# Two transformer blocks on one core: set-up and modulation sums moved into the second FFN, the last gates ahead of their gelu branch, weight splits at a raised priority

## The chip, the cores and the metric

The program runs on one core of a Trainium2 chip. The time is that of one execution on the device, in microseconds (us); lower is better. TensorE (PE) does matrix products, VectorE (DVE) and ScalarE (ACT) the elementwise work, GpSimd (POOL) set-up work, and SyncE (SP) issues most of the transfers from the chip's memory (DMA).

## The reference

A sequence of 256 positions with 1024 features, in float32, goes through a first block of two layers and then through a second block:

```python
for i in range(DEPTH):                       # first_block, DEPTH = 2
    h = rms_norm(x, norm_mix[i])
    x = x + (mixer_a(...) if i == 0 else mixer_b(...))
    h = rms_norm(x, norm_ffn[i])
    x = x + conv_ffn(h, f_w_up[i], f_conv_w[i], f_conv_b[i], f_w_down[i])
return rms_norm(x, norm_final)

mod = jax.nn.silu(c) @ ada_w[l] + ada_b[l]   # second_block
sh1, sc1, gt1, sh2, sc2, gt2 = jnp.split(mod[:, None, :], 6, axis=-1)
xn = _rmsnorm(h, mix_norm_g[l]) * (1.0 + sc1) + sh1
...                                          # sparse attention, a recurrence, gates
h = h + gt1 * (merged @ w_out[l])
xn2 = _rmsnorm(h, moe_norm_g[l]) * (1.0 + sc2) + sh2
h = h + gt2 * moe(xn2)                       # 32 experts
```

mixer_b is a gated linear recurrence: a gelu branch, a short convolution, two sigmoid gates per head, a scan, a projection out. conv_ffn projects 1024 features to 2 times 3072 (gate and value), runs a 3-tap convolution, multiplies gelu(gate) by value and projects back. The modulation `mod` has six vectors of 1024 (v = 0 to 5), which depend on the small input `c` alone and not on the sequence; v = 0 and 1 are wanted at the second mixer's start, v = 2 behind it, and v = 3, 4 and 5 at the experts.

## The kernel before

**Products.** Every weight is split into two parts of reduced precision, and one product becomes three matmuls (`mm3`, L272, L273, L274). A piece of weights is loaded into a ring of raw places (10 from the first FFN on), ACT copies its high part (L305), DVE subtracts to get the low part (L306), both into a ring of four split places (`arena_r_78` to `arena_r_81`; half-size pieces take `arena_r_82` and `arena_r_83` too). `wload` does this for each piece.

**Order.** The code is written once through; a tile scheduler gives each engine one fixed list of instructions, ranked by a priority that follows the order in which the code emits them. Each engine runs its list strictly in order. `tc.high_priority(n)` ranks what stands inside it as if it had been emitted n instructions earlier.

**Stages.** mixer_a, the first FFN, mixer_b, the second FFN, the final norm, the second mixer, the experts. An FFN has 13 steps: step s computes 256 gate and 256 value columns into the pool "ps" of PSUM (L272 and on), the convolution runs on DVE (L521), and gelu, product (L551) and split follow; from step 1 the projection back accumulates into the four banks of the pool "pc", which are all held until the FFN's ending. There the residuals (L420, four tiles) are added, the next norm's gain is multiplied (L1382 behind the second FFN), PE turns the tiles over (L377), and ACT sums squares (L334).

mixer_b runs four rounds P: `conv_in` (projection, convolution), `gelu_in` (the gelu branch), `recur` of the round before (L633 to L643: exp, tanh, sqrt and scans), `gates` (two gates per head, Tanh L621), then the projection out.

**Modulation.** `mod_load` loads a half vector of ada_w (4 loads of 0.5 MB on SP's queue). With `summed` DVE makes a weighted sum of eight rows (one L795, seven L797) into a buffer "msum", of which there are four; otherwise PE does that in `mod_steps` (L810, eight instructions per half). `mod_steps` then sums over the partitions on PE (L828 for v below 2 and v = 3 and 4, L817 for v = 2 and 5) into a bank of the pool "pc", which DVE adds to the bias (L830, L818):

```python
part = self.mod_scope.tile([128, 512], name="msum", bufs=4)
...
ps, by = psum(), self.sel4
...
ps, c0 = psum(), v * D + 512 * h
```

It handles whatever has been loaded since its last call: the FFNs call it at step 0, mixer_b at P = 0, and `final_norms` behind the second FFN. Before, v = 4 is loaded in mixer_b without `summed`, v = 3 and 5 in the second FFN with it.

**Set-up of block 2.** `setup2` stands between mixer_b and the second FFN: masks and tables (DVE L184, L888 to L905), a write of an image `x_img` and four small transposes on PE (L195, L909).

## Time and profile before

| | |
|---|---|
| time, median of 3 runs | 1501.51 us (1500.48 to 1504.97) |
| profiled execution: own time, span | 1502.12 us, 1500.4 us |
| granted TensorE clock, mean | 0.950 of 2.4 GHz |
| PE busy, share | 1371.2 us, 91% |
| DVE busy, share | 852.7 us, 57% |
| ACT busy, share | 615.2 us, 41% |
| POOL busy, share | 32.2 us, 2% |

The profiled execution is one run of the same program with the hardware profiler on; the span is the time from its first to its last instruction. A busy share is an average over all stages. In the profiled execution mixer_b runs from about 366 to 500 us, the second FFN from 508 to 727 us, the second mixer from 741 us and the experts from about 1040 us to the end.

### The profile page before, as it was taken

The numbers are of one execution on the slowest core, as the hardware profiler recorded it, in microseconds if no ns is written. First come the engines' busy times: TensorE is split into PE (matmuls) and PEld (weight loads), VectorE is DVE, ScalarE is ACT, GpSimd is POOL, SyncE is SP. The second block draws the span as 40 slices with busy tenths as digits, with TensorE's granted clock in tenths as the row PEclk, the third lists the DMA queues.
The fourth block names the chain that finished last, engine by engine and source line by source line (L and its number), as shares of the span: only waits on it lengthen the run. The fifth ranks groups of instructions, "written<-read, shape, count | busy, mean of one in ns | idle before, by whom it ended". The sixth has DMA issues, their size and how long they took to land.

```text
span 1500.4 us, 22885 instructions
## 1 busy us (share of the span) xinstructions
PE 1371.2 (91%) x9085; PEld 1042.1 (69%) x9085; DVE 852.7 (57%) x1628; ACT 615.2 (41%) x955; POOL 32.2 (2%) x63
## 2 busy tenths in 40 slices
PE   7999999999999899999999899998978878879785
PEld 6778999999998689999798688887413313234131
DVE  5796798778788789878859742775201101101011
ACT  6644555556688555555575544552100000000000
POOL 3000000000001000000000100001000000000000
PEclk9999999999999999999899795999999989999998
DMA  9898586555555578563243352487999999999997
GB/s 318 282 327 277 158 274 215 187 187 160 170 182 184 172 272 275 187 191 109 72 153 113 99 121 86 170 336 308 390 421 420 420 420 421 421 421 419 421 419 253
DMA packets 165573, 391.18 MB, mean 261 GB/s; under 512 B 19440, under 2 KB 101100, under 8 KB 141780
## 3 DMA queue, kind: packets, MB, share of 16 engines
q1 hardware_dynamic: 153124, 383.64, 70.2%
q10 hardware_dynamic: 11136, 4.53, 1.3%
q0 software_dynamic: 1200, 1.49, 0.4%
q8 instruction: 73, 1.20, 0.3%
q14 instruction: 40, 0.33, 0.1%
HBM read 386.19 MB, written 3.43 MB: 260 GB/s over the span
## 4 chain that ended last, share of the span: by engine, by line
PE 58%; DMA 29%; DVE 7%; ACT 4%; issue 2%; SPq 0%; POOL 0%; DVEq 0%; ACTq 0%
DMA arena<-expert_w_gate 12%; PE ps L272 9%; PE ps L273 9%; PE ps L274 9%; DMA arena_w<-expert_w_gate 7%; DMA arena_w<-expert_w_down 6%; PE pc L273 5%; PE pc L272 5%; PE pc L274 5%; DMA arena<-expert_w_down 3%; PE pg L272 2%; PE pg L274 2%; PE pg L273 2%; DVE arena_r L306 2%; ACT arena_r L305 1%
## 5 line engine op out<-in xcount | busy, mean ns | idle before, releaser
L305 ACT ACTIVATE arena_r<-arena 128x1024 fp32r<-128x1024 f32 (+2 forms) x330 | 328.9, 1008 | 287.1 <-PE ps L273 73.1
L306 DVE TENSOR_TENSOR arena_r<-arena,arena_r 128x1024 fp32r<-128x1024 f32 (+2 forms) x330 | 376.9, 1154 | 119.2 <-ACT arena_r L305 115.8
L272 PE MATMUL ps<-arena_r,arena_r 128*128 128x256 f32 (+2 forms) x1192 | 353.7, 297 | 1.0 <-DVE arena L818 1.0
L273 PE MATMUL ps<-arena_r,arena_r 128*128 128x256 f32 (+2 forms) x1192 | 352.9, 296 | 1.1 <-DVE arena_r L306 1.1
L274 PE MATMUL ps<-arena_r,arena_r 128*128 128x256 f32 (+2 forms) x1192 | 352.4, 296 | 0.6 <-DVE arena_r L306 0.6
L272 PEld LDWEIGHTS ps<-arena_r,arena_r 128*128 128x128 f32 (+1 forms) x1192 | 229.3, 192 | 10.4 <-issue 3.5
L273 PEld LDWEIGHTS ps<-arena_r,arena_r 128*128 128x128 f32 (+1 forms) x1192 | 229.2, 192 | 7.2 <-DVE arena_r L306 1.5
L274 PEld LDWEIGHTS ps<-arena_r,arena_r 128*128 128x128 f32 (+1 forms) x1192 | 229.2, 192 | 5.6 <-DVE arena_r L306 0.8
L1709 PE MATMUL pc<-arena 128*32 128x512 f32 x576 | 144.4, 672 | 34.1 <-DMA arena<-expert_w_up 18.9
L272 PE MATMUL pc<-arena_r,arena_r 128*128 128x512 f32 x344 | 136.0, 399 | 5.3 <-ACT arena_r L305 3.4
L273 PE MATMUL pc<-arena_r,arena_r 128*128 128x512 f32 x344 | 135.9, 395 | 0.4 <-DVE arena_r L306 0.4
L274 PE MATMUL pc<-arena_r,arena_r 128*128 128x512 f32 x344 | 134.2, 393 | 0.0
L1709 PE MATMUL pc<-arena_w,arena 128*32 128x512 f32 x448 | 117.4, 663 | 15.8 <-DMA arena_w<-expert_w_gate 9.8
L1716 DVE TENSOR_TENSOR arena<-arena,pc 128x512 f32<-128x512 f32 x8 | 5.5, 688 | 204.6 <-PE pc L1709 204.6
L1692 ACT ACTIVATE arena<-ps,mod_col,moe_g 128x128 f32<-128x128 f32 x32 | 14.7, 458 | 246.1 <-DVE arena L1694 246.1
L1709 PEld LDWEIGHTS pc<-arena 128*32 128x32 f32 x576 | 31.4, 120 | 99.1 <-issue 37.1
L272 PE MATMUL pg<-arena_r,arena_r 128*128 128x256 f32 (+1 forms) x312 | 95.0, 306 | 2.0 <-DVE arena L916 1.8
L273 PE MATMUL pg<-arena_r,arena_r 128*128 128x256 f32 (+1 forms) x312 | 94.7, 305 | 1.1 <-DVE arena_r L306 1.1
L274 PE MATMUL pg<-arena_r,arena_r 128*128 128x256 f32 (+1 forms) x312 | 95.1, 306 | 0.2 <-DVE arena_r L306 0.2
L521 DVE SCALAR_TENSOR_TENSOR arena<-arena 128x255 f32<-128x255 f32 (+2 forms) x228 | 94.4, 477 | 0.2
L1735 PE MATMUL pc<-arena 128*32 128x512 f32 (+2 forms) x320 | 74.7, 584 | 11.5 <-DMA arena<-expert_w_down 7.6
L272 PEld LDWEIGHTS pc<-arena_r,arena_r 128*128 128x128 f32 x344 | 65.2, 190 | 19.8 <-ACT arena_r L305 5.1
(451 smaller groups left out, 1688.2 us busy)
## 6 DMA issues: line engine op xcount, KB each, us to landing
arena<-f_w_up SPq DMA_DIRECT2D x96, 512.0 KB, 3.9
arena<-expert_w_gate SPq DMA_DIRECT2D x41, 1024.0 KB, 19.9
arena<-expert_w_down SPq DMA_DIRECT2D x34, 1024.0 KB, 19.9
arena_w<-expert_w_up SPq DMA_DIRECT2D x33, 1024.0 KB, 19.9
arena<-expert_w_up SPq DMA_DIRECT2D x31, 1024.0 KB, 19.9
arena_w<-expert_w_down SPq DMA_DIRECT2D x26, 1024.0 KB, 19.9
arena<-ada_w SPq DMA_DIRECT2D x48, 512.0 KB, 5.6
arena<-f_w_down SPq DMA_DIRECT2D x48, 512.0 KB, 4.2
```

What stands on the lines that cost most here:

```text
L272: nc.tensor.matmul(acc, ah, bh, start=first, stop=False, **kw)
L273: nc.tensor.matmul(acc, ah, bl, start=False, stop=False, **kw)
L274: nc.tensor.matmul(acc, al, bh, start=False, stop=last, **kw)
L305: self.nc.scalar.activation(hi, src, AF.Copy)
L306: self.nc.vector.tensor_tensor(lo, src, hi.bitcast(F32), ALU.subtract)
L521: nc.vector.scalar_tensor_tensor(o[:, i:], src[:, :S - i], w[k - 1 - i], o[:, i:], op0=ALU.mult, op1=ALU.add)
L1692: nc.scalar.activation(xg[:, k], ps[:, j], AF.Identity, scale=g, bias=sh)
L1709: nc.tensor.matmul(gu[i][es], xg[:, kk, es], ws[e][:, k], start=kk == 0, stop=kk == 7, skip_group_check=True)
L1716: tt(hd, hd, gu[1], ALU.mult)
L1735: nc.tensor.matmul(o[es], hT[:, k0 + k, es], ws[e][:, k, f0 - c0:f0 - c0 + n], start=k0 + k == 0, stop=k0 + k == 3, skip_group_check=True)
```

## The change

It does five things. (1) The two split instructions of `wload` are ranked 3000 places ahead. (2) In mixer_b's round P = 2 the gates are emitted ahead of the gelu branch. (3) mixer_b loads no modulation; v = 3, 4 and 5 are all loaded in the second FFN, all with DVE sums (v = 4 was summed on PE). (4) The second FFN calls `mod_steps` at steps 0, 6 and 12 instead of at 0 alone. (5) `setup2` is called at step 8 of the second FFN instead of ahead of it.

```diff
--- before.py
+++ after.py
@@ -216,7 +216,7 @@
         return t
 
 
-    PIECE, WPIECE = 1024, 2048
+    PIECE, WPIECE, URGENT = 1024, 2048, 3000
 
     def ring(self, raw, split):
 
@@ -252,7 +252,8 @@
             raw = self.load_raw(src[:, a0:a0 + m])
             o = self.place("split")
             parts = [view(self.ar.cols(o + i * self.PIECE, m * b), (m, b), F32R) for i in range(2)]
-            self.split_act(parts[0], parts[1], raw)
+            with self.tc.high_priority(self.URGENT):
+                self.split_act(parts[0], parts[1], raw)
             out += [(parts[0][:, i], parts[1][:, i]) for i in range(m)]
         return out
 
@@ -550,7 +551,7 @@
                     nc.scalar.activation(gf, gf, AF.Gelu_apprx_tanh)
                     nc.vector.tensor_tensor(gf, gf, vf, ALU.mult)
                     self.split_act(flat(hd[s][0]), flat(hd[s][1]), gf)
-                if s == 0:
+                if s in ((0,) if layer == 0 else (0, 6, 12)):
                     self.mod_steps()
                 if 1 <= s <= 10:
                     acc = acc or self.banks()
@@ -650,11 +651,14 @@
                     xb, xs = conv_in(P)
                 if P == 0:
                     self.mod_steps()
-                if P < 3:
+                if P < 2:
                     gg = gelu_in(P)
                 y = recur(P - 1, *todo, 4 if P < 3 else 2) if P > 0 else None
                 if P < 3:
-                    todo = (xb, gg, *gates(P, xs))
+                    rg = gates(P, xs)
+                    if P == 2:
+                        gg = gelu_in(P)
+                    todo = (xb, gg, *rg)
                 side(P)
                 if P > 0:
                     acc = acc or self.banks()
@@ -744,11 +748,16 @@
             ss = self.mixer_a(hT, ahead, factors, before, loads({2: (1, 0, 1), 3: (1, 1, 1)}), then(0))
             self.ring(10, 4)
             ss = self.ffn(hT, ss, 0, loads({1: (0, 0, 1), 3: (0, 1, 1), 6: (2, 0, 1), 9: (2, 1, 1)}), then(1))
-            ss = self.mixer_b(hT, ss, loads({0: (4, 0), 1: (4, 1)}), then(2))
-            self.setup2()
+            ss = self.mixer_b(hT, ss, lambda step: None, then(2))
             final, banks = Scope(self), []
-            ss = self.ffn(hT, ss, 1, loads({1: (3, 0, 1), 3: (3, 1, 1), 5: (5, 0, 1), 8: (5, 1, 1)}),
-                          lambda half: self.final_half(final, half, banks))
+            late = loads({1: (3, 0, 1), 2: (3, 1, 1), 3: (4, 0, 1), 4: (4, 1, 1), 6: (5, 0, 1), 7: (5, 1, 1)})
+
+            def beside(s):
+                late(s)
+                if s == 8:
+                    self.setup2()
+
+            ss = self.ffn(hT, ss, 1, beside, lambda half: self.final_half(final, half, banks))
             self.final_norms(final, ss, banks)
```

Lines of the changed kernel stand one further down from L256 on and nine further from L765 on: its L306 and L307 are L305 and L306 of before, L421 is L420, L635 to L644 stand for L634 to L643, L804 and L806 are L795 and L797, L837 and L839 are L828 and L830, L826 and L827 are L817 and L818, L1391 is L1382.

**DVE near the end of mixer_b.** The place is the last round's recurrence (L635), with the set-up of block 2 behind it; `arena` and `arena_r` are working storage and the split ring. Before:

```order
L184 MEMSET arena 128x128
L635 SCALAR_TENSOR_TENSOR arena<-arena 128x512
L306 TENSOR_TENSOR arena_r_79<-arena,arena_r_79 128x1024
L635 SCALAR_TENSOR_TENSOR arena<-arena 128x512
L306 TENSOR_TENSOR arena_r_80<-arena,arena_r_80 128x1024
L888 TENSOR_SCALAR arena<-m_d_4600,m_fr_4601 128x64
L889 TENSOR_SCALAR arena<-m_d_4600,m_fr_4601 128x64
L897 MEMSET arena 128x256
L893 CAST m_fr_4601<-m_ir_4599 128x1
L901 TENSOR_SCALAR arena<-m_d_4600,m_hi_4603 128x64
L894 TENSOR_SCALAR arena<-m_fr_4601 128x1
```

After, at the same recurrence (L636 there):

```order
L636 SCALAR_TENSOR_TENSOR arena<-arena 128x512
L806 SCALAR_TENSOR_TENSOR arena<-arena 128x512 x2
L307 TENSOR_TENSOR arena_r_79<-arena,arena_r_79 128x1024
L307 TENSOR_TENSOR arena_r_80<-arena,arena_r_80 128x1024
L307 TENSOR_TENSOR arena_r_83<-arena,arena_r_83 128x512
L806 SCALAR_TENSOR_TENSOR arena<-arena 128x512
L307 TENSOR_TENSOR arena_r_81<-arena,arena_r_81 128x1024
L636 SCALAR_TENSOR_TENSOR arena<-arena 128x512
L604 TENSOR_TENSOR arena<-ps_4261,arena 128x512
L806 SCALAR_TENSOR_TENSOR arena<-arena 128x512
L638 SCALAR_TENSOR_TENSOR arena<-arena 128x512
L806 SCALAR_TENSOR_TENSOR arena<-arena 128x512
```

The set-up's instructions (L888 and on) are gone from here, and modulation sums (L806) stand between the splits (L307) and the recurrence. In all, 28 such sums and the 4 that begin them (L804) stand between the first FFN's and mixer_b's residuals, where none stood; 19 and 2 of them come behind the first operation (L636) of round 1's recurrence. In the second FFN, which had 28 and 4, there remain 14 and 2.

**PE in step 0 of the second FFN.** `ps` is the FFN's product, `pc_4779` the norm factors spread over the partitions (L354), `pc_4803` the modulation v = 4 (L810, then L828). Before:

```order
L274 MATMUL ps_4644<-arena_r_76,arena_r_80 128x256
L354 MATMUL pc_4779<-arena,ones 128x128
L810 MATMUL pc_4803<-arena 32x512
L354 MATMUL pc_4779<-arena,ones 128x128
L810 MATMUL pc_4803<-arena 32x512 x7
L272 MATMUL ps_4843<-arena_r_76,arena_r_81 128x256
L273 MATMUL ps_4843<-arena_r_77,arena_r_81 128x256
L274 MATMUL ps_4843<-arena_r_76,arena_r_81 128x256
L272 MATMUL ps_4843<-arena_r_76,arena_r_81 128x256
L273 MATMUL ps_4843<-arena_r_77,arena_r_81 128x256
L274 MATMUL ps_4843<-arena_r_76,arena_r_81 128x256
L828 MATMUL pc_4813<-arena 64x1 x8
```

After:

```order
L275 MATMUL ps_4570<-arena_r_76,arena_r_80 128x256
L355 MATMUL pc_4705<-arena,ones 128x128
L273 MATMUL ps_4729<-arena_r_76,arena_r_81 128x256
L274 MATMUL ps_4729<-arena_r_77,arena_r_81 128x256
L275 MATMUL ps_4729<-arena_r_76,arena_r_81 128x256
L273 MATMUL ps_4729<-arena_r_76,arena_r_81 128x256
L355 MATMUL pc_4705<-arena,ones 128x128
L274 MATMUL ps_4729<-arena_r_77,arena_r_81 128x256
```

The 16 instructions of L810 are gone altogether; the 16 of L828 for v = 4 are gone from here and stand at the end of the second FFN, so that 32 of them stand there instead of 16: 16 between its last ten matmuls and 16 behind them. The five transposes of `setup2` (L195, L909), which stood directly ahead of the first matmul of this FFN, now stand some 950 rows further down.

**DVE at the end of the second FFN.** `pc_4972` and `pc_4974` of before and `pc_4860` of after are the FFN's last accumulators. Before:

```order
L420 TENSOR_TENSOR arena<-arena,pc_4973 128x512
L1382 TENSOR_TENSOR arena<-arena 128x512
L420 TENSOR_TENSOR arena<-arena,pc_4972 128x512
L1382 TENSOR_TENSOR arena<-arena 128x512
L420 TENSOR_TENSOR arena<-arena,pc_4974 128x512
L830 TENSOR_TENSOR mod_col<-mod_col,pc_6736 64x8
L1382 TENSOR_TENSOR arena<-arena 128x512
L830 TENSOR_TENSOR mod_col<-mod_col,pc_6746 64x8
L306 TENSOR_TENSOR arena_r_78<-arena,arena_r_78 128x864
```

After, from the first addition into `mod_col` but one:

```order
L307 TENSOR_TENSOR arena_r_78<-arena,arena_r_78 128x864
L839 TENSOR_TENSOR mod_col<-mod_col,pc_5709 64x8
L839 TENSOR_TENSOR mod_col<-mod_col,pc_5719 64x8
L806 SCALAR_TENSOR_TENSOR arena<-arena 128x512
L307 TENSOR_TENSOR arena_r_80<-arena,arena_r_80 128x888
L839 TENSOR_TENSOR mod_col<-mod_col,pc_5729 64x8
L806 SCALAR_TENSOR_TENSOR arena<-arena 128x512
L804 TENSOR_SCALAR arena<-arena 128x512
L806 SCALAR_TENSOR_TENSOR arena<-arena 128x512 x10
L421 TENSOR_TENSOR arena<-arena,pc_4860 128x512
L806 SCALAR_TENSOR_TENSOR arena<-arena 128x512
L1391 TENSOR_TENSOR arena<-arena 128x512
```

Ahead of the last residual (L421 with `pc_4860`) there now stand all four additions into `mod_col` (L839) and most of the sums of v = 5 (L804, L806); before, it stood ahead of both additions and had no sums near it.

Beside these: ACT has three more table loads in mixer_b; its third weight split at the kernel's start stands ahead of the first normalised block (L366); and in the second mixer some matmuls change places.

## Rows read from the trace of the kernel before

**Rows 1.** Windows: busy us (instructions) of each engine, clock, DMA share, GB/s.

```profile
366.00:440.00 74.00, 73.42 (x563) 69.44 (x562) 63.33 (x110) 57.11 (x92) 0.00 (x0) 1.00 0.51 158
440.00:500.00 60.00, 56.24 (x359) 49.83 (x358) 51.26 (x81) 46.22 (x65) 5.65 (x11) 1.00 0.62 202
500.00:508.00 8.00, 4.85 (x25) 2.97 (x25) 6.83 (x20) 6.76 (x16) 0.00 (x0) 0.94 0.56 187
508.00:534.00 26.00, 26.00 (x181) 20.58 (x181) 13.68 (x39) 9.67 (x13) 0.00 (x0) 0.89 0.62 206
534.00:728.00 194.00, 193.98 (x1344) 181.43 (x1344) 166.88 (x242) 108.98 (x143) 2.58 (x6) 0.99 0.58 188
741.00:1040.00 299.00, 279.80 (x2493) 249.94 (x2494) 190.33 (x466) 155.59 (x297) 11.88 (x13) 0.89 0.51 169
```

**Rows 2.** Waits of PE in mixer_b, 366 to 500 us: total, times, longest.

```profile
PE pc L272 <- ACT arena_r L305: 3.4, 2, 1.7
...
PE pc L273 <- DVE arena_r L306: 0.4, 1, 0.4
```

**Rows 3.** Timeline of ACT at the start: start us, us, what [idle before <-releaser].

```profile
10.40 1.06 ACT L305 ACTIVATE arena_r<-arena 128x1024 fp32r<-128x1024 f32 x1 [0.66 <-DMA arena<-a_w_in]
```

**Rows 4.** Modulation sums on DVE: one timeline row, two source rows (ns min/median/max).

```profile
570.11 2.07 DVE L797 SCALAR_TENSOR_TENSOR arena<-arena 128x512 f32<-128x512 f32 x3
...
L797 DVE SCALAR_TENSOR_TENSOR arena<-arena x70: 737/746/756, 77.0 to 611.2; 128x512 f32<-128x512 f32 x70
...
L795 DVE TENSOR_SCALAR arena<-arena x10: 478/482/489, 61.9 to 585.4; 128x512 f32<-128x512 f32 x10
```

**Rows 5.** Timeline of DVE at the set-up of block 2 in mixer_b.

```profile
480.92 0.26 DVE L888 TENSOR_SCALAR arena<-m_d,m_fr 128x64 f32<-128x64 f32 x1 [1.97 <-DMA x_img<-arena]
```

**Rows 6.** Timeline of ACT at a table load in mixer_b.

```profile
423.07 1.28 ACT L604 ACT_TABLE_LOAD   x1
424.36 0.63 ACT L604 ACTIVATE arena<-arena 128x512 f32<-128x512 f32 x1
```

**Rows 7.** Timeline of PE at the step into the second FFN.

```profile
503.74 0.25 PE L195 MATMUL ps<-ident,arena 43*128 43x43 f32 x1
504.03 0.53 PE L909 MATMUL ps<-ident,arena 128*8 128x128 f32 x2
507.08 0.76 PE L909 MATMUL ps<-ident,arena 128*8 128x128 f32 x2 [2.52 <-DVE arena_r L367]
```

**Rows 8.** Timeline of PE in step 0 of the second FFN.

```profile
520.15 0.28 PE L272 MATMUL ps<-arena_r,arena_r 128*128 128x256 f32 x1
...
520.82 1.04 PE L810 MATMUL pc<-arena 128*32 128x512 f32 x2
...
522.22 1.92 PE L810 MATMUL pc<-arena 128*32 128x512 f32 x14
...
526.98 3.18 PE L810 MATMUL pc<-arena 128*32 128x512 f32 x16
...
531.37 2.08 PE L828 MATMUL pc<-arena 128*64 128x1 f32 x16
...
535.13 0.41 PE L274 MATMUL ps<-arena_r,arena_r 128*128 128x256 f32 x1
```

**Rows 9.** Timeline of PE at the end of the second FFN.

```profile
726.89 0.40 PE L274 MATMUL pc<-arena_r,arena_r 128*128 128x512 f32 x1
...
727.66 3.55 PE L828 MATMUL pc<-ones,arena 128*64 128x1 f32 x32
...
740.84 0.55 PE L272 MATMUL ps<-arena_r,arena_r 128*128 128x256 f32 x1 [1.01 <-DVE arena L818]
```

**Rows 10.** Timeline of DVE at the end of the second FFN.

```profile
727.33 0.69 DVE L420 TENSOR_TENSOR arena<-arena,pc 128x512 f32<-128x512 f32 x1 [0.74 <-PE pc L274]
...
729.85 0.68 DVE L1382 TENSOR_TENSOR arena<-arena 128x512 f32<-128x512 f32 x1
...
731.44 1.06 DVE L306 TENSOR_TENSOR arena_r<-arena,arena_r 128x864 fp32r<-128x864 f32 x1
```

## The prediction

> **What bounds the kernel now.** I read the page first, then a table of windows by stage, the waits of TensorE (PE), and the timelines at the places that the change touches. The page's shares (PE 91%, the vector engine, DVE, 57%) hide the stages. The table of windows [rows 1] shows PE full in the second FFN (26.00 of 26 us from 508 to 534, 193.98 of 194 us from 534 to 728), nearly full in the first 74 us of mixer_b (73.42), and with holes at the end of mixer_b (56.24 of 60 us) and at the step into the second FFN (4.85 of 8); the step out of it, 14 us without an FFN matmul, is in a timeline [rows 9]. In mixer_b DVE is busy for 63.33 of 74 and then 51.26 of 60 us, so it is close to being a second bound there. In the second FFN it is busy for 166.88 of 194 us and PE does not wait: there work taken off PE is therefore time, and work taken off DVE is not. The expert stage behind is bound by transfers, but its loads are released by PE's work ahead of it, so I count a shift of PE before the experts one to one at the end.
>
> All terms are made against the profiled execution: its own time is 1502.12 us, its span 1500.4 us; the median of the runs shown is 1501.51 us, so 0.6 us comes off at the end. A plus is slower.
>
> **The change, part by part.**
>
> *Weight splits first.* In mixer_b PE waits for the two halves of a split: 3.4 us in two waits for the ACT copy (L305) and 0.4 us for the DVE subtract (L306) [rows 2]. Splits that go ahead of other work can remove these: 3.8 us, less if DVE is late anyway. At the kernel's start the third split now stands ahead of the first normalised block, L366, on ACT. One such copy is 1.06 us and before it ACT waited 0.66 us for its weights [rows 3], so the first matmul comes 0 to 1.7 us later; I take +1.3, nearer to the full price.
>
> *Modulation sums of v=3 and v=4 in mixer_b.* The order of after has 28 of the seven-per-half L797 and 4 of the one-per-half L795 between mixer_b's start and its first residual, where before had none of them: they were summed in the second FFN (v=3) or on PE (v=4). A run of three L797 takes 2.07 us, of which the third needs 0.75, so the pitch is 0.66; an L795 is 0.48 alone, and I take 0.40 by the same overlap [rows 4]. The set-up's DVE work leaves mixer_b: L888 (0.26 us) and ten small ones behind it and a memset, some 2 us (an estimate from the first row, with overlap), and with them a wait of 1.97 us for the write of x_img [rows 5].
> In the last 60 us DVE idles 60 − 51.26 = 8.7 us; 19 of the L797 and 2 of the L795 now stand there, 19 × 0.66 + 2 × 0.40 = 13.3 us. The idle time and the 2 us removed hold 10.7, so DVE is late by 2.6 us even if it never waits. It will wait: it depends on ACT and PE in this stretch. Of the idle time, 1.97 us is the x_img wait that goes; of the remaining 6.8 I keep half, 3.4 us. DVE's end of mixer_b, and with it the residual that PE's next transposes need, is then 2.6 + 3.4 = 6.0 us late. Against this stands the 3.8 us of split waits that no longer hold up PE's chain: +2.2. The bounds are −3.8 (all sums fit) and +13.3 (none does). The other 9 L797 and 2 L795, 6.7 us, meet 74 − 63.33 = 10.7 us of idle DVE and cost nothing. Their loads move too: 8 loads of ada_w, 0.5 MB each, leave the second FFN for mixer_b's part of SP's queue. There 0.62 of the engines' time moves 202 GB/s [rows 1], so full engines would move some 326 (an estimate) and 4 MB need 13 us; 0.38 of 60 us and 0.49 of 74 are free, 59 us, and I cost them at nothing.
>
> *Gates ahead of the last gelu branch.* The same matmuls in another order, and three more activation table loads on ACT, 1.28 us each [rows 6], 3.8 us. ACT is idle for 60 − 46.22 = 13.8 us in the last 60 us, so I cost them at nothing; without that cover they would be 3.8.
> The Trainium skill ("ScalarE: Activation LUTs", section on what a table load costs) puts a switch of tables at about 2.66 us, 1.28 of it the load and the rest a drain, and advises to group by table, which speaks against this edit. The trace agrees with the 1.28 but shows the activation 0.01 us behind the end of the load [rows 6]: no drain there. By the page's figure the three would be an estimated 8.0 us.
>
> *Set-up of block 2 moves behind.* At the step into the second FFN PE waits 2.52 us ahead of the last two of the L909 transposes [rows 7]; the four L909 and the L195 are gone from there. The matmuls then run at the lower clock of 1.2 GHz: 0.41 us instead of 0.28 for each record [rows 8], from 507.73 to about 510.4; PE had been idle for 3.15 of the 8 us around it. At the full rate these 2.7 us would be about half; without the hole I take 1.2 us back: −3.7 together (bounds −1.0 and −5.6). Inside the FFN the same five transposes cost their own 0.25 + 0.53 + 0.76 us: +1.5 (bounds +1.0, and +4.0 if the 2.5 us wait comes with them).
>
> *Modulation v=4 off PE.* In step 0 of the second FFN PE runs 32 records of L810, 1.04 + 1.92 + 3.18 us, and 32 of L828 in two groups of 2.08 us each [rows 8]. Spans overlap by 0.1 or 0.2 us, so L810 is 5.9 us and L828 4.0. PE is full there: −9.9. A second low-clock stretch follows, with matmuls of 0.41 us from 534.5 to 537.7 [rows 8]; with dense matmuls ahead of it in place of thin ones, it goes: −1.5. Together −11.4, the surest term (bounds −9.9 to −12).
>
> *The tail of the second FFN.* The code asks for the modulation steps at s=6 and s=12, but the FFN's accumulators hold all four banks of the pool until its ending, so the order puts the L828 of v=3 and v=4 between and behind the last matmuls: 4.0 us more on PE, last FFN matmul at 726.89 + 4.0 = 730.9 instead of 726.89 [rows 9]. The sums of v=5 need the buffers (four of "msum") that these L828 free, so DVE's order puts 14 L797 and 2 L795 at the tail, most of them ahead of the last residual L420. What is late is thus this chain: last L828 of 32 records (3.55 us) behind 730.9 and four transposes of 0.60 us ends at 735.0; the fourth L830 at 735.3; then 11 L797 and an L795, 7.7 us, so the last residual starts at 743.0 instead of 727.33; its product L1382 ends at 745.0 instead of 730.5 (before, it stood behind an L830; [rows 10]). From there the sums, the final norm and the first matmul of the second mixer follow as before, which was at 740.84 [rows 9]. That is +14.4; the splits that now run while DVE waits take 1.06 us, and a shorter one, off the chain at most [rows 10]. I take +13 (bounds +11 and +15).
>
> *Second mixer.* PE's order differs in some places through the scheduler. Its idle time there is 299 − 279.80 = 19.2 us [rows 1]; no row prices the new order, and I bound it by ±6, a third of that, and take nothing.
>
> **Sum:** 1.3 + 2.2 − 3.7 + 1.5 − 11.4 + 13 = +2.9, so 1505.0 by the own time and 1504.4 by the median. A measurement of this kernel tells about 0.3%, or 4.5 us, from no change.
>
> **The rivals.**
> *Faster: the sums hide.* If mixer_b's DVE fills its gaps, the term there is −3.8 instead of +2.2, and the rest stands: 1498.4; with the tail at +11 it is 1496.4, and with a second mixer that gains its 6 as well 1490. For it: 19.4 us of idle DVE in mixer_b against 20 of new sums. Against it: the gaps in the last 60 us are short, and waits for ACT. It decides at a DVE lateness under 3 us at mixer_b's first residual.
> *Slower: DVE becomes mixer_b's bound.* With strict order, each sum that stands ahead of a split or a scan delays it. If nothing of the last 13.3 us is hidden, the term is +13.3 and the time 1515.5; half way 1510. It decides when DVE shows no idle time from 440 on and PE waits for L306 or L420. Before, the second FFN carried 32 such sums, and PE did not wait for them in its 194 us [rows 1], which speaks against the extreme.
> *The second mixer's order* gives or costs its 6: 1498 or 1510.
> *Table loads with a drain.* With 8.0 us on ACT instead of 3.8, 13.8 us of idle ACT still hold it unless the gates' Tanh stands ahead of PE's next split; then 4.2 more, 1508.6. The Trainium skill's page named above is the source of that rule; on the rows I give it 0.04.
> *The change doesn't do what it says* for the modulation steps inside the FFN; that is in the forecast, as the tail.
>
> **Chances.** The forecast 0.38 (1499 to 1509; faster 0.03, same 0.25, slower 0.10), the sums hide 0.28 (faster 0.21, same 0.07), DVE's bound 0.20 (slower 0.18, same 0.02), the second mixer's order 0.10 (faster 0.04, slower 0.06), table loads 0.04 (same 0.02, slower 0.02). Faster 0.28, same 0.36, slower 0.36. The time is that of the forecast, 1504. The range, 1491 to 1516, takes in the second mixer's gain below and an unhidden mixer_b above; the forecast's own is 1499 to 1509.
>
> **What would show it.** In the profile after: no L810; first FFN matmul right behind the transposes and no half-clock stretch near 534; the second FFN's first 26 us about 10 us shorter; last FFN matmul to first second-mixer matmul about 23 us instead of 14; DVE ahead of the last residual in a run of sums; mixer_b as long as before within 5 us. The prediction fails if DVE's run at the tail starts before the L830, if mixer_b grows by over 8 us, or if the second mixer changes by more than 6.

## The result: 1.4% slower, and the profile after

The changed kernel took 1522.87 us (median of 4 runs, 1522.36 to 1525.26) against 1501.14 us before (4 runs): ratio 1.0143, 95% interval 1.0122 to 1.0163, so 21.7 us slower where 1504 was forecast and 1516 was the end of the range. The span of its profiled execution is 1520.7 us, 20.3 more than before.

First, where it went. The table gives for each trace how much later than before the same event is, in us, so each column's step over the one to its left is that stage's own loss. The events: mixer_a's first residual (before at 153.36), the first FFN's last product (362.27), the second FFN's first matmul (507.73) and last (726.89), the second mixer's first matmul (740.84), the first expert matmul (1047.76), the end of the span. The stretch from the second FFN's last matmul to the second mixer's first is called the tail below.

| kernel | mixer_a | FFN 1 | FFN 2 first | FFN 2 last | 2nd mixer first | experts first | end |
|---|---|---|---|---|---|---|---|
| changed | +6.2 | +6.5 | +9.8 | +3.5 | +14.3 | +18.3 | +20.3 |
| e1_urgent | +6.4 | +6.7 | +13.2 | +12.4 | +11.9 | +21.6 | +23.2 |
| f1_first | +7.2 | +7.6 | +14.2 | +10.5 | +10.4 | +13.1 | +14.7 |
| f2_second | +0.1 | +0.2 | −0.2 | −1.5 | −1.9 | +7.0 | +8.8 |
| f_u30 | +3.0 | +3.0 | +6.9 | +5.6 | +5.5 | +8.8 | +8.5 |
| g1_act | +0.4 | +0.4 | +4.2 | +2.8 | +4.6 | +9.1 | +10.6 |
| g2_dve | +0.1 | +0.3 | +8.1 | +6.8 | +7.2 | +12.0 | +13.6 |
| e2_gates | +0.3 | +0.3 | +1.8 | +1.2 | +0.7 | +0.8 | +0.2 |
| e4_mod | −0.7 | −0.7 | +2.9 | −8.8 | +3.8 | +2.0 | +1.6 |
| e6_nourgent | +1.0 | +1.1 | −1.0 | −7.3 | +0.8 | −2.2 | −2.7 |
| e5_ps | +7.9 | +8.3 | +14.1 | +17.9 | +17.4 | +23.1 | +22.6 |
| e7_psnu | 0.0 | 0.0 | −1.0 | −0.8 | −2.8 | −7.0 | −7.0 |
| e8_psnug | +1.8 | +1.8 | −0.8 | −1.2 | −3.2 | −1.9 | −2.2 |

Each row is one execution, and single stages vary: e7_psnu and e8_psnug, which differ in mixer_b's gates alone, are 1.8 us apart in mixer_a and 5.5 in the second mixer. A step of 2 or 3 us in one row alone says little.

In the changed kernel the second FFN gains 6.3 us to its last matmul and its tail gives back 10.8. The forecast was +2.9 and the trace has +20.3. Of the 17.4 us between them 5.2 stand up to the first FFN's last product, 3.6 from there to the second FFN's first matmul, 0.8 in that FFN, 1.8 in its tail, 4.0 in the second mixer and 2.0 in the experts.

The table of windows of the changed kernel, by the same stages as [rows 1] (columns as there):

```profile
373.00:447.00 74.00, 70.86 (x548) 66.85 (x547) 67.17 (x119) 55.68 (x87) 0.00 (x0) 1.00 0.63 198
447.00:510.00 63.00, 58.58 (x358) 51.64 (x357) 62.52 (x86) 50.39 (x68) 0.62 (x2) 0.97 0.78 258
510.00:518.00 8.00, 5.65 (x34) 4.50 (x33) 6.98 (x14) 6.80 (x16) 0.49 (x1) 1.00 0.89 312
518.00:544.00 26.00, 26.00 (x200) 25.65 (x200) 19.65 (x47) 15.11 (x21) 0.00 (x0) 0.93 0.51 159
```

The second FFN's first 26 us are at clock 0.93 (0.89 in [rows 1]). DVE in the last part of mixer_b is busy for 62.52 of 63 us, where it was 51.26 of 60. A full DVE alone does not make mixer_b late, though: e6_nourgent, below, has it busy for 129.84 of mixer_b's 135 us, and its second FFN starts 1.0 us early.

In mixer_a a part of the loss is PE's clock. These are the windows around 60 to 110 us, first of the kernel before, then of the changed one:

```profile
60.00:110.00 50.00, 47.67 (x217) 38.46 (x216) 49.57 (x109) 25.12 (x30) 0.00 (x0) 1.00 0.95 331
```

```profile
62.00:112.00 50.00, 45.84 (x200) 37.33 (x199) 47.54 (x114) 23.50 (x29) 0.00 (x0) 0.93 0.89 314
...
88.00:96.00 8.00, 6.56 (x22) 4.99 (x21) 7.28 (x14) 1.19 (x2) 0.00 (x0) 0.57 0.99 354
```

And PE in the changed kernel there:

```profile
87.52 0.41 PE L388 MATMUL ps<-ident,arena 128*128 128x128 f32 x2 [2.71 <-DVE arena L491]
...
92.22 0.63 PE L275 MATMUL ps<-arena_r,arena_r 128*128 128x512 f32 x1
```

PE waits 2.71 us for DVE, then the granted clock stands at 0.57 from 88 to 96 us, mostly at the lower level of 1.2 GHz, and a matmul of 128x512 takes 0.63 us instead of 0.39 (at 96.37, with the clock back). From 13 to 17 us, behind the wait at the start, the clock is 0.60. Before, it was 1.00 in both places.

The timeline of PE at the end of the second FFN, as [rows 9]:

```profile
725.69 2.08 PE L837 MATMUL pc<-ones,arena 128*64 128x1 f32 x16
...
728.36 2.08 PE L837 MATMUL pc<-ones,arena 128*64 128x1 f32 x16
730.37 0.64 PE L275 MATMUL pc<-arena_r,arena_r 128*128 128x512 f32 x1
...
731.79 3.55 PE L837 MATMUL pc<-ones,arena 128*64 128x1 f32 x32
743.21 1.86 PE L826 MATMUL pc<-arena,ones 128*1 128x512 f32 x2 [7.87 <-DVE arena L806]
...
755.10 1.01 PE L273 MATMUL ps<-arena_r,arena_r 128*128 128x256 f32 x3 [0.36 <-ACT arena_r L1417]
```

And DVE there, as [rows 10]:

```profile
727.80 0.15 DVE L839 TENSOR_TENSOR mod_col<-mod_col,pc 64x8 f32<-64x8 f32 x1 [2.05 <-PE pc L837]
...
735.75 0.17 DVE L839 TENSOR_TENSOR mod_col<-mod_col,pc 64x8 f32<-64x8 f32 x1
...
737.02 6.71 DVE L806 SCALAR_TENSOR_TENSOR arena<-arena 128x512 f32<-128x512 f32 x10
743.76 0.69 DVE L421 TENSOR_TENSOR arena<-arena,pc 128x512 f32<-128x512 f32 x1
...
745.03 0.68 DVE L1391 TENSOR_TENSOR arena<-arena 128x512 f32<-128x512 f32 x1
```

The last residual (L421) stands at 743.76 behind ten sums in a row that begin at 737.02, and PE waits 7.87 us for sums of v = 5. From the last FFN matmul (730.37) to the second mixer's first (755.10) it is 24.7 us instead of 13.95; 23 were expected.

The waits of PE from mixer_b to the second FFN's start (total, times, longest), as [rows 2]:

```profile
PE ps L273 <- DVE arena_r L368: 4.0, 2, 2.0
PE ps L273 <- ACT arena_r L306: 3.0, 2, 1.6
PE pc L273 <- ACT arena_r L306: 1.2, 2, 0.8
```

The L909 transposes and their wait are gone from the entrance, but PE now waits 2.0 us ahead of each of two stages (mixer_b's first matmul and the second FFN's) for DVE's normalised block (L368); the waits for the splits' ACT copies are 4.2 us where 3.4 were to go away. At the second FFN's start DVE in the changed kernel has two weight splits between the last residual (L421, ended at 514.76) and the block:

```profile
514.67 2.35 DVE L307 TENSOR_TENSOR arena_r<-arena,arena_r 128x1024 fp32r<-128x1024 f32 x2
516.94 1.26 DVE L368 SCALAR_TENSOR_TENSOR arena_r<-ps,arena,arena_r 128x256 fp32r<-128x256 f32 x3
```

In e6_nourgent, the changed kernel without the raised priority (below), the block comes first and the split behind it, and PE has neither of the two waits:

```profile
504.88 1.28 DVE L420 TENSOR_TENSOR arena<-arena,pc 128x512 f32<-128x512 f32 x2
506.17 0.88 DVE L367 SCALAR_TENSOR_TENSOR arena_r<-ps,arena,arena_r 128x256 fp32r<-128x256 f32 x2
506.96 1.22 DVE L306 TENSOR_TENSOR arena_r<-arena,arena_r 128x1024 fp32r<-128x1024 f32 x1
```

### The profile page after: what moved, and what is told of

Read it like the earlier page. It is cut to its first block, busy times and chain, and to the rows that moved or that the text cites. A ratio compares the mean times of both kernels' runs of the same rounds, so it can differ in the third digit from the quotient of the medians.

```text
span 1520.7 us, 22854 instructions
## 1 busy us (share of the span) xinstructions
PE 1369.4 (90%) x9053; PEld 1039.8 (68%) x9053; DVE 867.5 (57%) x1644; ACT 621.0 (41%) x956; POOL 32.5 (2%) x63
## 4 chain that ended last, share of the span: by engine, by line
PE 58%; DMA 29%; DVE 8%; ACT 2%; issue 1%; SPq 0%; DVEq 0%; ACTq 0%
DMA arena<-expert_w_up 9%; PE ps L273 9%; PE ps L274 9%; PE ps L275 9%; DMA arena_w<-expert_w_up 8%; DMA arena<-expert_w_down 6%; PE pc L273 5%; PE pc L275 5%; PE pc L274 5%; DVE arena_r L307 3%; DMA arena_w<-expert_w_down 3%; PE pg L273 2%; PE pg L275 2%; PE pg L274 2%; PE pc L1718 1%
## 5 line engine op out<-in xcount | busy, mean ns | idle before, releaser
L307 DVE TENSOR_TENSOR arena_r<-arena,arena_r 128x1024 fp32r<-128x1024 f32 (+2 forms) x330 | 377.0, 1156 | 141.3 <-ACT arena_r L306 131.7
L306 ACT ACTIVATE arena_r<-arena 128x1024 fp32r<-128x1024 f32 (+2 forms) x330 | 329.3, 1007 | 301.8 <-PE ps L274 80.2
L273 PE MATMUL ps<-arena_r,arena_r 128*128 128x256 f32 (+2 forms) x1192 | 353.6, 298 | 7.4 <-DVE arena_r L368 4.0
L274 PE MATMUL ps<-arena_r,arena_r 128*128 128x256 f32 (+1 forms) x1192 | 353.6, 297 | 0.9 <-DVE arena_r L307 0.9
L275 PE MATMUL ps<-arena_r,arena_r 128*128 128x256 f32 (+1 forms) x1192 | 352.7, 296 | 0.0
L273 PEld LDWEIGHTS ps<-arena_r,arena_r 128*128 128x128 f32 (+1 forms) x1192 | 229.1, 193 | 15.7 <-DVE arena_r L368 4.5
L274 PEld LDWEIGHTS ps<-arena_r,arena_r 128*128 128x128 f32 x1192 | 229.7, 193 | 7.4 <-DVE arena_r L307 1.3
L275 PEld LDWEIGHTS ps<-arena_r,arena_r 128*128 128x128 f32 x1192 | 229.5, 193 | 5.2
L1701 ACT ACTIVATE arena<-ps,mod_col,moe_g 128x128 f32<-128x128 f32 x32 | 14.7, 459 | 246.9 <-DVE arena L1703 246.9
L1744 PE MATMUL pc<-arena 128*32 128x512 f32 (+2 forms) x320 | 74.3, 572 | 13.4 <-DMA arena<-expert_w_down 9.4
```

The costliest lines, as they stand in the source:

```text
L273: nc.tensor.matmul(acc, ah, bh, start=first, stop=False, **kw)
L274: nc.tensor.matmul(acc, ah, bl, start=False, stop=False, **kw)
L275: nc.tensor.matmul(acc, al, bh, start=False, stop=last, **kw)
L306: self.nc.scalar.activation(hi, src, AF.Copy)
L307: self.nc.vector.tensor_tensor(lo, src, hi.bitcast(F32), ALU.subtract)
L1701: nc.scalar.activation(xg[:, k], ps[:, j], AF.Identity, scale=g, bias=sh)
```

## The experiments

**The priority alone, and everything but it.** Theory A: the raised priority of the splits is what costs. Theory B: the moved work does.

e1_urgent, onto the kernel before:

```diff
-            self.split_act(parts[0], parts[1], raw)
+            with self.tc.high_priority(3000):
+                self.split_act(parts[0], parts[1], raw)
```

> The kernel before with the raised priority of the weight splits as its only edit. Theory A (the priority itself costs time: it pushes the norm and mixer_a's small work behind splits, and costs again at the step into mixer_b and in the second mixer): the first residual of mixer_a at about 159.5 us as in the changed kernel (before 153.4), the whole at 1508 to 1513 us. Theory B (the priority costs only its 1.4 us at the start; the other lateness ahead of the second FFN comes from set-up work and modulation sums that were moved): first residual at about 154.8, the whole at 1501 to 1504 us.

Measured: 1520.96 us, ratio 1.0129 (1.0111 to 1.0147); mixer_a's first residual at 159.72. Theory A, and more than it asked for: one edit makes nearly the whole loss.

e6_nourgent takes those lines out of the changed kernel.

> The changed kernel without the raised priority (gates, modulation and set-up as changed). Theory A: first residual of mixer_a back at about 153.4 us, the step into the second FFN some 7 us earlier than in the changed kernel, the tail of the second FFN as there (about 24 us from the last FFN matmul to the first matmul of the second mixer), the whole at 1510 to 1516 us. Theory B: 1519 to 1523 us, first residual within 2 us of 159.5.

Measured: 1499.59 us, ratio 0.9984 (0.9972 to 0.9997); mixer_a's first residual at 154.39, 1.0 late, and the tail 22.1 us (719.56 to 741.67). The place was as theory A said; the size was not: the other four parts together do not cost, they gain some 2.4 us (0.4 to 4.2 by the interval). Theory B fell. In the presence of the other four the priority costs more than alone: some 23 us by the medians (1522.87 against 1499.59). By the table, 5.2 of them stand in mixer_a, 5.4 in mixer_b and the entrance of the second FFN, 2.6 in the tail, 7.0 in the second mixer and 2.5 in the experts.

**The tail repaired.** e5_ps lets the steps at 6 and 12 use the pool that the FFN's products rotate through:

```diff
                 if s in ((0,) if layer == 0 else (0, 6, 12)):
-                    self.mod_steps()
+                    self.mod_steps(self.psum if s else None)
```

> The changed kernel, but the modulation steps at s = 6 and 12 take their bank from the pool of the FFN's products (ps) instead of the one that the accumulators hold, so the sums over partitions run inside the FFN, and the sums of v = 5 need not wait for the tail. If the chain of held banks, held msum buffers and sums ahead of the last residual is what the tail costs: about 13 to 15 us from the last FFN matmul to the first of the second mixer (24.7 in the changed kernel), the FFN itself up to 4 us longer by the matmuls that it takes in, the whole 9 to 14 us below the changed kernel, 1509 to 1514 us. Rival (the second mixer's first matmul is held by something else, its norm or its loads): tail over 20 us, within 4 us of 1522.9.

Measured: 1522.19 us, ratio 1.0132 (1.0113 to 1.0152), no gain. The tail is 13.4 us (744.81 to 758.25), so the chain that was named is what the tail costs; but the FFN from first to last matmul is 223.0 us instead of 212.9. The forecast of this run failed because it let the FFN take in 4 us. The moved matmuls' own time, by the spacing of PE's records, is near that: 2.9 us for the 16 L837 that stood behind the last matmul, 1.8 for the four records of L826. Another 2.4 are longer waits at the set-up's transposes (2.0 and 0.8 us). The remaining 3 us or so are the FFN's own matmuls, which run at the lower clock behind the thin ones:

```profile
630.55 5.02 PE L837 MATMUL ps<-ones,arena 128*64 128x1 f32 x48
```

```profile
633.00:644.00 11.00, 11.00 (x57) 9.22 (x57) 3.98 (x9) 0.67 (x1) 0.00 (x0) 0.53 0.17 51
```

From 633 to 644 us the granted clock is 0.53, and a matmul of 128x512 takes 0.63 us there instead of 0.39. The rival's number came out, its reason did not.

e7_psnu is the same without the raised priority.

> Both repairs: no raised priority, and the modulation steps at s = 6 and 12 on banks of the products' pool. Theory A: the costs add up, so 1498 to 1503 us, first residual at about 153.4 and a tail of 13 to 15 us. Theory B (the lateness ahead of the second FFN is from the moved work): 1508 to 1514 us.

Measured: 1495.62 us, ratio 0.9962 (0.9949 to 0.9975): faster than both kernels, and below theory A's 1498 to 1503. The tail is 11.9 us (726.12 to 738.06) and the FFN 219.4; the windows of this kernel, columns as in [rows 1]:

```profile
507.00:726.00 219.00, 218.90 (x1524) 203.00 (x1524) 175.42 (x280) 119.00 (x162) 2.42 (x6) 0.98 0.50 161
726.00:738.00 12.00, 5.01 (x33) 3.49 (x31) 10.70 (x52) 6.92 (x14) 0.00 (x0) 0.63 0.46 128
```

PE is full in the FFN with all the sums over partitions in it (218.90 of 219 us), and in the tail DVE works on the norm without sums (10.70 of 12).

Against e6_nourgent the repair is worth 4.0 us: 10.2 from the tail, 6.5 given back in the FFN, both from the traces.

**Where the priority costs.** Theory H: each stage pays, since a split pushed far ahead waits at the head of its engine's queue and holds up short work behind it. Rival K: the second mixer alone. f1_first and f2_second raise the priority in one half of the program:

```diff
-            with self.tc.high_priority(3000):
+            with self.tc.high_priority(3000) if self.urgent else nullcontext():
```

> The kernel before with the raised priority of the weight splits in the first block alone (mixer_a to the second FFN); the second mixer's splits as before. Theory H (a split that is pushed far ahead stands at the head of its engine's queue, waits there for its ring place or its copy, and holds up the short work behind it; each stage pays for its own): the lateness at the second mixer's first matmul as with the priority everywhere, about +12 us, and no more from there: 1511 to 1515 us. Rival K (one place carries it all, the second mixer's long serial chain): 1501 to 1504 us.

Measured: 1515.51 us, ratio 1.0085 (1.0066 to 1.0104); at the second mixer's first matmul +10.4.

> The counterpart: the raised priority in the second mixer alone. Theory H: no change up to 741 us, then +8 to +12 us between the second mixer's first matmul and the experts, 1509 to 1513 us. Rival K: 1518 to 1522 us, nearly the whole loss. Rival M (the second mixer suffers only because it starts late against its loads): within 3 us of before.

Measured: 1513.46 us, ratio 1.0076 (1.0060 to 1.0093), −1.9 at the second mixer's first matmul, +7.0 at the experts' first and +8.8 at the end. Both halves pay for themselves; K and M fell. The two losses add to 25 us where both together lose 19, so they overlap, in part by lateness carried on (f1_first loses another 4.3 us behind 741).

f_u30 writes 30 for 3000.

> The kernel before with the splits ranked 30 places ahead instead of 3000, so that a split passes its neighbours but not whole stages of short work. Theory H: most of the loss is gone, 1499 to 1507 us. Rival O (any split ahead of the small chain work costs, however far it is moved, since the engines are nearly full): over 1512 us.

Measured: 1509.61 us, ratio 1.0046 (1.0029 to 1.0063): between the two. Passing 30 neighbours already costs 40% of it, so "pushed past whole stages" is not the whole cause.

**Waiting or displacing.** Theory D: a moved split costs by its own length, on an engine that is locally full. Rival W: by its wait for a ring place. g1_act and g2_dve raise one of the two instructions:

```diff
-        self.nc.scalar.activation(hi, src, AF.Copy)
-        self.nc.vector.tensor_tensor(lo, src, hi.bitcast(F32), ALU.subtract)
+        with self.tc.high_priority(up) if up else nullcontext():      # g1_act; in g2_dve around the other
+            self.nc.scalar.activation(hi, src, AF.Copy)
+        self.nc.vector.tensor_tensor(lo, src, hi.bitcast(F32), ALU.subtract)
```

> The kernel before with the raised priority on the ACT copy of each weight split alone; the DVE subtract keeps its place. Theory D (a split that is moved forward displaces, by its own 1.1 us, chain work on an engine that is locally full; DVE is the fuller engine in mixer_a and in the second mixer's serial chain, ACT only in the end of mixer_b): less than half of the whole edit's loss, 1503 to 1510 us, with most of it in mixer_b. Rival W (the copies at the head of ACT's queue wait for ring places, and that wait holds up what is behind): over 1513 us.

> The counterpart: raised priority on the DVE subtract alone, the ACT copy as before. Theory D: the larger part, 1508 to 1518 us, with mixer_a and the second mixer late. Rival W: the subtract follows a copy that is no earlier, so little: 1500 to 1506 us.

Measured: 1514.11 us (ratio 1.0087, 1.0073 to 1.0102) and 1514.44 us (1.0079, 1.0065 to 1.0094). Each costs about 12 us: g1_act came out as W had it (over 1513), g2_dve as D had it (1508 to 1518), so the runs do not part the two. Mixer_a's 6 us appear with neither alone (+0.4, +0.1) and only with both. PE's waits ahead of L388 (L389 in these two kernels) are shorter with one of them, 2.0 and 1.8 us against 3.6, and the clock from 88 to 96 us stays at 1.00. f_u30 has waits of 3.9 us there with the clock at 1.00, and mixer_a is 3.0 us late; e1_urgent, f1_first and the changed kernel have such waits and a clock of 0.57 to 0.61, and are 6 to 7 us late. By this comparison about half of mixer_a's loss goes with the waits and half with the clock; why the clock fell behind the same wait in three kernels and not in f_u30 is open.

The traces part them in some places. At the step into the second FFN, shown above, DVE does two splits without a gap while PE waits for the block behind them: that is displacement. The second mixer has a serial chain of short operations on DVE that ends in a reciprocal root, for which PE waits. In the changed kernel, timeline of DVE, the chain's first operation (L1008), the splits inside it (L307) and its last (L323), then PE's matmul behind it:

```profile
828.15 0.17 DVE L1008 TENSOR_SCALAR arena<-pc 128x16 f32<-128x16 f32 x1 [0.25 <-PE pc L1006]
828.24 1.22 DVE L307 TENSOR_TENSOR arena_r<-arena,arena_r 128x1024 fp32r<-128x1024 f32 x1
...
832.42 1.21 DVE L307 TENSOR_TENSOR arena_r<-arena,arena_r 128x1024 fp32r<-128x1024 f32 x1
...
835.09 1.23 DVE L307 TENSOR_TENSOR arena_r<-arena,arena_r 128x1024 fp32r<-128x1024 f32 x1 [0.34 <-ACT arena_r L306]
...
838.07 1.23 DVE L307 TENSOR_TENSOR arena_r<-arena,arena_r 128x1024 fp32r<-128x1024 f32 x1
...
840.78 1.22 DVE L307 TENSOR_TENSOR arena_r<-arena,arena_r 128x1024 fp32r<-128x1024 f32 x1
...
843.47 1.22 DVE L307 TENSOR_TENSOR arena_r<-arena,arena_r 128x1024 fp32r<-128x1024 f32 x1
...
845.99 1.22 DVE L307 TENSOR_TENSOR arena_r<-arena,arena_r 128x1024 fp32r<-128x1024 f32 x1
...
848.63 0.16 DVE L323 SCALAR_TENSOR_TENSOR arena<-arena 128x16 f32<-128x16 f32 x1
```

```profile
848.85 0.38 PE L1013 MATMUL pc<-ident,arena 128*8 128x128 f32 x2 [3.99 <-DVE arena L323]
```

In e6_nourgent, which differs from it by the priority alone, the same rows (L1007, L306, L322, and PE's L1012):

```profile
815.76 0.17 DVE L1007 TENSOR_SCALAR arena<-pc 128x16 f32<-128x16 f32 x1 [0.63 <-PE pc L1005]
...
816.25 1.22 DVE L306 TENSOR_TENSOR arena_r<-arena,arena_r 128x1024 fp32r<-128x1024 f32 x1
...
827.32 1.22 DVE L306 TENSOR_TENSOR arena_r<-arena,arena_r 128x1024 fp32r<-128x1024 f32 x1
...
828.54 1.22 DVE L306 TENSOR_TENSOR arena_r<-arena,arena_r 128x1024 fp32r<-128x1024 f32 x1
829.67 0.17 DVE L322 SCALAR_TENSOR_TENSOR arena<-arena 128x16 f32<-128x16 f32 x1
```

```profile
830.09 0.38 PE L1012 MATMUL pc<-ident,arena 128*8 128x128 f32 x2
```

The chain takes 20.6 us with seven splits inside and 14.1 us with three. Four more splits of 1.22 us are most of the 6.6 us, and only one of the seven was waited for, 0.34 us: here they displace, as theory D has it. PE had run out of other matmuls by then and waited 3.99 us; without the priority it did not wait. The fourteen traces agree on this place: the kernels in which the subtract is raised in the second mixer at 3000 places (changed, e1_urgent, e5_ps, f2_second, g2_dve) have seven splits inside the chain, 20.4 us or more, and a wait of PE of 3.8 or 4.0 us; the kernel before and all others have two or three, 14.1 us or less, and no wait. It is not the second mixer's whole loss: f_u30 and g1_act lose 3.2 and 4.6 us there without it.

In mixer_a the same shows in the waits of PE (total, times, longest), before for L490, in e1_urgent for the same operation, L491:

```profile
PE ps L387 <- DVE arena L490: 1.2, 2, 0.7
```

```profile
PE ps L388 <- DVE arena L491: 3.6, 2, 2.5
```

In one place both show. At 468.50 PE of the changed kernel waits 1.60 us for an activation's split. On DVE a weight split of 1.2 us stands ahead of the convolution that feeds it; on ACT the weight split ahead of it has waited 1.86 us for its ring place, and holds it up by another 0.9. How much of the loss elsewhere is displacement and how much waiting was not measured.

**The single parts.** e4_mod makes the modulation's edits alone.

> The kernel before with the change of the modulation alone (v = 3 to 5 in the second FFN with DVE sums, steps at 0, 6 and 12); set-up, gates and priority as before. By the prediction's terms: mixer_b +2 to +4, the entrance of the second FFN unchanged, step 0 about -11, the tail +8 to +14 through PE's wait for the sums of v = 5: 1500 to 1506 us, last residual not behind the sums since the order has it ahead of them. Rival (sums in mixer_b make DVE its bound): mixer_b +8 or more and 1508 to 1515 us.

Measured: 1504.12 us, ratio 1.0015 (1.0002 to 1.0027): as the terms had it. From mixer_a's first residual to the second FFN's first matmul +3.5, in it −11.6, in the tail +12.6.

e2_gates emits the gates of P = 2 first.

> The kernel before with the gates of round P = 2 ahead of their gelu branch as the only edit. As predicted the three table loads lie in ACT's idle time: within 3 us of before, first FFN matmul of layer 1 within 3 us of 507.7. Rival (ACT is in mixer_b's chain, and table loads are on it): first FFN matmul 4 to 8 us late, 1505 to 1510 us.

Measured: 1502.98 us, ratio 1.0008 (0.9999 to 1.0017), the second FFN's first matmul 1.8 us late: no change, as predicted.

e8_psnug is e7_psnu without the gates' edit.

> The modulation and set-up edits with the banks of the products' pool, no raised priority, gates as before. If the gates' edit costs nothing or little, as fast as with it, 1493 to 1498 us. If it gains: 1498 to 1501. If it costs what three table loads are, 1490 to 1493.

Measured: 1496.86 us, ratio 0.9964 (0.9950 to 0.9977): the gates' edit is worth nothing that these runs can show. This and e7_psnu beat the kernel before by 0.4%.

## Why the prediction was wrong

**The step that failed** is the first: "Splits that go ahead of other work can remove these: 3.8 us". It took the waits that PE has for splits as the upper bound of what the order of the splits can do, and priced the other side at the start of the kernel alone.

It also misread the 3.4 us of [rows 2]. L305 and L306 are lines of a helper, which splits weights and activations alike, and only the splits of `wload` are raised. A piece of weights in mixer_b has 1024 columns; both waits are for copies of 512 columns (at 486.05 and 494.40), the split of the recurrence's product (L643, split at L644). Before, ACT's copy and the matmul that waits for it:

```profile
486.05 0.63 ACT L305 ACTIVATE arena_r<-arena 128x512 fp32r<-128x512 f32 x1 [0.68 <-DVE arena L643]
```

```profile
486.73 0.49 PE L272 MATMUL pc<-arena_r,arena_r 128*128 128x512 f32 x1 [1.71 <-ACT arena_r L305]
```

In e1_urgent the same two, with the product at L644:

```profile
499.70 0.63 ACT L306 ACTIVATE arena_r<-arena 128x512 fp32r<-128x512 f32 x1 [0.23 <-DVE arena L644]
```

```profile
500.38 0.80 PE L273 MATMUL pc<-arena_r,arena_r 128*128 128x512 f32 x1 [4.46 <-ACT arena_r L306]
```

So the waits were for work that the edit puts behind the weights, not ahead. From the last round's first exp to this copy ACT does three weight splits before and six in e1_urgent, and PE's wait grows from 1.71 to 4.46 us; f1_first, f_u30 and g1_act have six there too, and waits of 4.5 to 4.7. In the changed kernel the waits of 4.2 us are again for 512-column splits. (For the same reason `arena_r_82` and `arena_r_83`, written there with 512 columns, hold activations and no weights.)

In general, to move a split ahead of other work is to move other work behind a split. On ACT and DVE, whose lists are strictly in order, that other work was the short serial operations for which PE waits next. The priority alone loses 19 us (e1_urgent), and 23 beside the other edits. The forecast had +1.3 at the start (measured: the copies at 10.46 and 11.82 ahead of L367, first matmul 1.4 us late) and −3.8 in mixer_b.

```profile
10.46 1.06 ACT L306 ACTIVATE arena_r<-arena 128x1024 fp32r<-128x1024 f32 x1 [0.40 <-DMA arena<-a_w_in]
11.82 1.06 ACT L306 ACTIVATE arena_r<-arena 128x1024 fp32r<-128x1024 f32 x1 [0.30 <-DMA arena<-a_w_in]
12.78 0.82 ACT L367 ACTIVATE arena_r<-ps,g_a 128x256 fp32r<-128x256 f32 x2
```

The same step left mixer_a and the second mixer uncounted: "no row prices the new order, and I bound it by ±6, a third of that, and take nothing". The second mixer was +4.0, 7.0 more than in e6_nourgent, and mixer_a +4.8 beyond the start. It could have been priced: the chain ahead of PE's L1004 has seven splits of 1.22 us inside it after the change and three before. None of the prediction's three signs of failure came (the sums began behind the L839, mixer_b's last residual is 7.0 us later against the one ahead of it, the second mixer changed by 4.0): they did not watch mixer_a.

**What was right.** The other terms are read against e6_nourgent, which is the change without that edit:

| term | forecast | measured |
|---|---|---|
| mixer_b (to its last residual) | +2.2 | +3.7 |
| entrance of the second FFN, to its first matmul (the 2.5 of the −3.7) | −2.5 | −4.1 |
| second FFN, first to last matmul (−1.2 − 11.4 + 1.5 + 4.0) | −7.1 | −6.3 |
| tail, last matmul to second mixer's first (13 − 4.0) | +9 | +8.2 |
| second mixer, to the experts' first matmul | 0 | −3.0 |

Mixer_b's figure is the last residual's lateness, +3.1, less that of the residual ahead of mixer_b, −0.7 (371.48 against 372.16). Counted from the first FFN's last product, it is +2.0. The term came out near by luck, by two errors that cancel: its 3.8 us for the priority are not in this kernel, so the forecast for it is +6.0, and DVE's lateness was 3.7 and not 6.0. In the changed kernel the same count is +7.0, and +3.3 from the first FFN's last product to the second FFN's first matmul. The rival "DVE becomes mixer_b's bound" is met in part only: DVE is full there, but it is as full in e6_nourgent, and the difference between the two goes with the two waits for L368. The second mixer's −3.0 is inside what single traces vary by.

In step 0 L810 and the second low-clock stretch went as said; the windows of e6_nourgent show mixer_b with its full DVE, the second FFN's first 26 us at clock 1.00 and the second mixer at the 0.89 of before:

```profile
372.00:507.00 135.00, 129.42 (x910) 119.63 (x911) 129.84 (x206) 105.46 (x155) 1.11 (x2) 0.99 0.69 226
507.00:533.00 26.00, 26.00 (x208) 25.44 (x208) 23.32 (x54) 18.69 (x29) 0.00 (x0) 1.00 0.65 217
...
742.00:1046.00 304.00, 285.58 (x2530) 256.24 (x2533) 194.48 (x483) 157.31 (x302) 12.14 (x13) 0.89 0.53 175
```

The rival of the table loads with a drain did not appear: e2_gates, with two loads more than before (19 instead of 17), is no slower. The changed kernel has three more. The chance of 0.36 for "slower" was mostly given to mixer_b and the second mixer's order; its largest cause, the priority, was not among the rivals.

## What to carry to other kernels

Where engines run fixed lists, a raised priority is a swap, not a gift: before giving it to a frequent 1 us operation, list what it passes on each engine, and count how many of them come to stand inside each serial chain of short operations. Work that needs a resource which a stage holds to its end (PSUM banks, a buffer ring) runs at that stage's end wherever the code asks for it; giving it another pool moves it, but on a full engine it then costs its own time there, and here some 3 us more by the lower clock behind it. A wait put down to a line of a helper must be traced to its caller, by shape and releaser, before an edit of one caller is priced by it. A sum of terms can be near in four and wrong in one: run the change without each part.

## What was not expected of the hardware's traces

Raising either instruction of a split alone costs as much as two thirds of raising both (1514.1 and 1514.4 against 1521.0 us, before 1502), and neither shows the 6 us of mixer_a that both together do. The experts' stage adds another 1.5 to 2 us in six of the eight kernels whose first expert matmul is 7 us late or more (f2_second +7.0 to +8.8), but nothing in f_u30 and e5_ps; why was not tried.
